# Seven block products in phases of two and five, and one more matrix group of each feed-forward computed that way

## The chip, the cores and the metric

The program runs on one core of a Trainium2 chip. The metric is device time in microseconds of one execution; lower is better. The kernel before takes 2251.7 us (median of three runs, 2251.38 to 2252.15).

## The reference

The reference is one layer of a decoder on 256 rows of 2048 float32 values: a feed-forward block, a token mixer, and a second feed-forward block. The change touches the two feed-forward blocks only. Each computes, with `D_FF` = 5504:

```
def swiglu(x, w_gate, w_up, w_down):
    return (jax.nn.silu(x @ w_gate) * (x @ w_up)) @ w_down
...
    h = swiglu(rms_norm(x, ffn1_pre[l]), ffn1_wg[l], ffn1_wu[l], ffn1_wd[l])
    x = x + 0.5 * rms_norm(h, ffn1_post[l])
```

## The kernel before

All matrix products run on TensorE (PE) in a reduced float32 format. To keep float32 accuracy each operand is split into a high and a low part, and a product is three matmuls: high by high, high by low, low by high. The activations are split once; the weights come from memory as plain float32 (`raw` tiles of 128 x 1024, 512 KB), and for each tile ScalarE (ACT) writes the high part `whi` (L168) and VectorE (DVE) subtracts it to get the low part `wlo` (L169). There are 12 `raw` buffers and 5 pairs of `whi`/`wlo`, so ACT and DVE can be at most five tiles ahead of PE. PSUM has eight banks (`acc`, `tp`), each of 512 columns.

The 43 column tiles of 128 in `D_FF` are worked in five groups of eight (f = 0, 8, 16, 24, 32) and a last group of three. For a group there is a gate product (with `wg`), an up product (with `wu`), the product of both, its transposition (`split_T`, eight transposes on PE a row block, then a split by ACT and DVE into `hh`, `hl`), and a down product (with `wd`) whose partial sums are added in memory (`ysum`, by DMAs of the POOL queue).

A plain product (`linear_steps`) of a group's 1024 columns needs 192 matmuls of 512 columns for the 256 rows. The gate groups f = 8 to 32 use `seven` instead: rows and columns are cut into halves, and the four block products of each quarter are had from seven instead of eight products of sums of blocks, M1 to M7, 168 matmuls. The sums of the activations (`forms`, tiles `sh`, `sl`) are made once. The sums of weight blocks are made per tile: by DVE additions in place (L420, L424), and one by a DMA that adds while it lands (L428, POOL queue). The products run in `phase`s; a phase works on several products side by side, in four steps s = 0 to 3 of two contraction tiles each, and each product holds a PSUM bank until it is done and folded into the results `c0`, `c1`. Before, the phases are M1, M5, M6, M4 and then M3, M2, M7.

`seven` yields after each weight tile (6 matmuls). `weave` takes steps of a main sequence (up and down of group f, 12 matmuls a weight tile) and lets the seven products of the next gate group run in between, in a fixed ratio of matmuls. So the order on each engine is fixed when the program is built; the queues are then worked in order. Loads are issued by the SP queue in that order too. After the woven groups come the up product of f = 32 (plain, two chunks of 512 columns at once) and gate and up of the last three column tiles (one loop with two chunks of 384 columns), both unwoven, and last the down product of the remaining eleven tiles, whose results go through the norm (`closer`).

The functions that are changed, with the line numbers of the profile:

Of the kernel before, what the change touches and what calls it, by code (L numbers as in the profile page):

```python
# [11 lines left out]
F32R = mybir.dt.float32r  # L12
I32 = mybir.dt.int32
AF = mybir.ActivationFunctionType
# [40 lines left out]
def layer(ctx: ExitStack, tc: tile.TileContext, a, out: bass.AP):  # L55
# [17 lines left out]
    def tmp(shape, s="t"):  # L73
        return pool.tile(shape, F32, tag="tmp", bufs=N_TMP, name=nm(s))
# [183 lines left out]
        for _ in linear_steps(*args, **how):  # L258
            pass

    def weave(main, side, ratio):

        credit = 0.0
        for n in main:
            credit += n * ratio
            while side is not None and credit >= 0:
                n = next(side, None)
                if n is None:
                    side = None
                else:  # L270
                    credit -= n
        for n in side or ():
            pass

    def linear_steps(lhs, wts, evac, head=2, tail=4, by_chunk=None, before=None, ahead=None):

        nk, chunks, span, parts = wts.nk, wts.chunks, wts.span, wts.parts
        batches = [min(head, nk)]
        while sum(batches) < nk:
            left = nk - sum(batches)
            batches.append(left if left <= tail else min(2, left - tail))
        ps = [None, None]
        k0 = 0
        for bi, nb in enumerate(batches):
            last = bi == len(batches) - 1
            if before is not None:  # L290
                before(k0)
            wts.need(k0 + nb)
            if last and ahead is not None:
                ahead()
            for t in range(2):
                if bi == 0:
                    while t and pending:
                        pending.pop(0)()
                    ps[t] = [acc(w) for _, _, w in chunks]
                whole = [list(range(len(chunks)))]  # L300
                for cs in ([[c] for c in whole[0]] if last and by_chunk else whole):
# [77 lines left out]
    def seven(forms, W, col, evac):  # L379


        c0, c1 = slot([P, 1024], F32, "sg"), slot([P, 1024], F32, "sg")
        a, b = slice(0, 512), slice(512, 1024)

        def src(i, j, s):
            k = 8 * i + 2 * s
            return W[k * P:(k + 2) * P, col + 512 * j:col + 512 * j + 512].rearrange("(k p) c -> p k c", p=P)

        def load(i, j, s):
            x = raw_tile()  # L390
            nc.sync.dma_start(out=x.rearrange("p (k c) -> p k c", c=512), in_=src(i, j, s))
            return x

        def phase(plan):

            bank = {}
            seen = {p: 0 for p, _, _ in plan}
            for _, p, s, operand in sorted((len(plan) * s + d, p, s, o) for s in range(4) for p, d, o in plan):
                x = operand(s)
                hi, lo = split_tiles()  # L400
                split(hi, lo, x)
                if p not in bank:
                    bank[p] = acc(512)
                ah, al = forms[p]
                for i in range(2):
                    k, ws = 2 * s + i, slice(512 * i, 512 * i + 512)
                    PE.matmul(bank[p], ah[:, k, :], hi[:, ws], start=(seen[p] == 0), stop=False)  # L407
                    PE.matmul(bank[p], ah[:, k, :], lo[:, ws], start=False, stop=False)  # L408
                    PE.matmul(bank[p], al[:, k, :], hi[:, ws], start=False, stop=(seen[p] == 7))  # L409
                    seen[p] += 1  # L410
                yield p if seen[p] == 8 else 0, bank[p]

        xs, es, ys = {}, {}, {}

        def b11(s):
            xs[s], es[s], ys[s] = load(0, 0, s), load(0, 1, s), load(1, 1, s)
            return xs[s]

        def t1(s):
            V.tensor_tensor(xs[s], xs[s], es[s], ALU.add)  # L420
            return xs[s]

        def t2(s):
            V.tensor_tensor(xs[s], xs[s], ys[s], ALU.add)  # L424
            return xs[s]

        def t4(s):
            G.dma_start(out=xs[s].rearrange("p (k c) -> p k c", c=512), in_=src(1, 0, s), accum_op=ALU.add)  # L428
            return xs[s]

        for p, ps in phase([(1, 0, b11), (5, 2.1, t1), (6, 4.2, t2), (4, 8.3, t4)]):
            if p == 1:
                S.activation(c0[:, a], ps, AF.Copy)
            elif p == 5:
                m5 = ps
            elif p == 6:
                q = tmp([P, 512], "q")
                V.tensor_tensor(q, c0[:, a], ps, ALU.subtract)
                V.tensor_tensor(c1[:, b], q, m5, ALU.add)
            elif p == 4:  # L440
                V.tensor_tensor(c1[:, a], q, ps, ALU.add)
            yield 6

        def b22(s):
            xs[s], es[s] = load(1, 1, s), load(0, 1, s)
            return xs[s]

        def b21(s):
            return load(1, 0, s)

        for p, ps in phase([(3, 0, b22), (2, 1, b21), (7, 2.1, t1)]):
            if p == 3:
                V.tensor_tensor(c0[:, b], c1[:, b], ps, ALU.add)
            elif p == 2:
                V.tensor_tensor(c0[:, a], c0[:, a], ps, ALU.add)
            elif p == 7:
                V.tensor_tensor(c1[:, b], c1[:, b], ps, ALU.add)
                V.tensor_tensor(c1[:, a], c1[:, a], ps, ALU.add)
            yield 6
        evac([c0, c1])  # L460
# [107 lines left out]
    def ffn(u, r, first, head, wg, wu, wd, gpost, resid, keep, gname, final, unscale=None):  # L568
# [15 lines left out]
        def chunks(W, f, n):  # L584
            return [(W, c * P, min(512, (f + n - c) * P)) for c in range(f, f + n, 4)]

        def both_later(todo):
            def later():
                for x in todo:
                    x()  # L590

            return later

        def gate_plain(t, ps, f):
            sg[f][t] = slot([P, 1024], F32, "sg")
            for i, p in enumerate(ps):
                S.activation(sg[f][t][:, i * 512:i * 512 + p.shape[-1]], p, AF.Silu, scale=scale(t))
# [21 lines left out]
        def up_steps(f):  # L619
            for i in (0, 4):  # L620
                yield from linear_steps(lu, Weights(KD, [(wu, (f + i) * P, 512)]), lambda t, ps, i=i: up(t, ps[0], f, i, 4))
# [19 lines left out]
        last = n_tile // BLOCK * BLOCK  # L641
        sg = {f: {} for f in range(0, n_tile, BLOCK)}
        forms = {}
        weave(linear_steps(lu, first, lambda t, ps: gate_plain(t, ps, 0), head=head), new_forms(u, forms), 0.5)
        for f in range(0, last, BLOCK):
            if f + BLOCK < last:
                main = itertools.chain(up_steps(f), down_steps(f))
                weave(main, seven(forms, wg, (f + BLOCK) * P, lambda c, f=f + BLOCK: gate_seven(c, f)), 168 / 384)
            else:
                linear(lu, Weights(KD, chunks(wu, f, BLOCK)), lambda t, ps, f=f: both_later([up(t, ps[i], f, 4 * i, 4) for i in range(2)]))  # L650

        def both(t, ps):
            gate_plain(t, ps[:1], last)
            return up(t, ps[1], last, 0, n_tile - last)

        linear(lu, Weights(KD, chunks(wg, last, n_tile - last) + chunks(wu, last, n_tile - last)), both)
        y = [[slot([P, 1024], F32, "y") for _ in range(2)] for _ in range(2)]
        begin, chunk, post, un, rn, sq, _ = closer(y, gpost, 0.5, resid, keep, gname, final, None, unscale)
        f0 = last - BLOCK
        for half in range(2):  # L660
            for t in range(2):
                G.dma_start(out=y[t][half], in_=ysum[t * P:(t + 1) * P, half * 1024:(half + 1) * 1024])
# [504 lines left out]
```

## Time and profile before

| | |
|---|---|
| median of three runs | 2251.7 us |
| the profiled execution | 2252.43 us, span of its instructions 2250.6 us |
| mean granted TensorE clock | 0.993 of full speed |
| busy: PE, weight loads (PEld), DVE, ACT, POOL | 98%, 84%, 67%, 53%, 6% of the span |
| first feed-forward, from its first woven group to its last product | about 85 to 771 us of the span |
| second feed-forward, likewise | about 1564 to 2231 us |

A busy share is the time in which an engine had an instruction running. The durations of single matmuls in the profile are modelled and overlap each other, so the time that one costs is read from the starts of neighbours, not from its own duration.

### The profile page before, as it was taken

What the parts mean: (1) busy time and instruction counts of PE and PEld (TensorE: products, weight loads), DVE (VectorE), ACT (ScalarE), POOL (GpSimd) and SP (SyncE); (2) the same over time, 40 slices, a digit from 0 to 9 for tenths busy, and PEclk for the clock granted to TensorE, in tenths of its full rate; (3) what the DMA queues carried; (4) which work ended last, traced back from release to release, by engine and by line L of the source; (5) the groups of instructions that cost most, each with busy time, mean ns of one, the idle gap of its engine ahead of it and who ended that gap; (6) DMA issues with size and microseconds to landing.
All of it is one profiled execution on the core that took longest, in us unless ns stands there. A gap on an engine that the chain in (4) does not pass through costs nothing.

```text
span 2250.6 us, 28724 instructions
## 1 busy us (share of the span) xinstructions
PE 2211.6 (98%) x10482; PEld 1884.0 (84%) x10482; DVE 1511.4 (67%) x1797; ACT 1203.4 (53%) x1534; POOL 128.7 (6%) x169
## 2 busy tenths in 40 slices
PE   8899999999999999999999999999999999999997
PEld 6788888888889799999888888887888888888896
DVE  5777777767755758676555545558777777776556
ACT  7655556565544654545444444456555565555444
POOL 1000001010000000000000000000000010000100
PEclk9999999999999999999999999999999999999999
DMA  8578889898977464456655566755788898989871
GB/s 301 182 225 271 271 250 280 246 281 257 260 258 260 151 209 128 147 158 179 198 186 189 187 196 204 234 181 172 243 262 277 241 287 246 285 253 273 280 229 54
DMA packets 230016, 505.83 MB, mean 225 GB/s; under 512 B 19129, under 2 KB 52113, under 8 KB 229873
## 3 DMA queue, kind: packets, MB, share of 16 engines
q1 hardware_dynamic: 206400, 448.91, 61.0%
q0 software_dynamic: 23296, 55.00, 11.6%
q8 instruction: 82, 1.34, 0.2%
q14 instruction: 62, 0.50, 0.1%
q10 hardware_dynamic: 176, 0.07, 0.0%
HBM read 480.83 MB, written 23.07 MB: 224 GB/s over the span
## 4 chain that ended last, share of the span: by engine, by line
PE 51%; DVE 1%; ACT 1%; issue 0%; DVEq 0%
PE acc L307 14%; PE acc L308 14%; PE acc L310 14%; PE acc L407 2%; PE acc L409 2%; PE acc L408 2%; PE tp L175 1%; ACT junk L164 0%; ACT uh L186 0%; DVE y L548 0%; DVE raw L352 0%; DVE wlo L169 0%; PE tp L1037 0%; DVE y L526 0%; ACT whi L168 0%
## 5 line engine op out<-in xcount | busy, mean ns | idle before, releaser
L169 DVE TENSOR_TENSOR wlo<-raw,whi 128x1024 fp32r<-128x1024 f32 (+2 forms) x914 | 1068.0, 1180 | 601.5 <-ACT whi L168 576.8
L168 ACT ACTIVATE whi<-raw 128x1024 fp32r<-128x1024 f32 (+2 forms) x914 | 931.1, 1028 | 820.4 <-PE acc L310 675.4
L307 PE MATMUL acc<-whi,uh 128*128 128x512 f32 (+1 forms) x1752 | 657.8, 377 | 11.3 <-ACT whi L168 10.5
L308 PE MATMUL acc<-wlo,uh 128*128 128x512 f32 (+1 forms) x1752 | 652.6, 374 | 2.6 <-DVE wlo L169 2.0
L310 PE MATMUL acc<-whi,ul 128*128 128x512 f32 (+1 forms) x1752 | 555.5, 373 | 0.0
L307 PEld LDWEIGHTS acc<-whi,uh 128*128 128x128 f32 x1752 | 330.0, 189 | 58.8 <-ACT whi L168 12.3
L308 PEld LDWEIGHTS acc<-wlo,uh 128*128 128x128 f32 x1752 | 330.3, 189 | 50.3 <-DVE wlo L169 3.9
L310 PEld LDWEIGHTS acc<-whi,ul 128*128 128x128 f32 x1752 | 326.4, 189 | 46.6
L307 PE MATMUL acc<-whi,hh 128*128 128x512 f32 x688 | 268.9, 391 | 0.0
L308 PE MATMUL acc<-wlo,hh 128*128 128x512 f32 x688 | 267.9, 389 | 0.0
L310 PE MATMUL acc<-whi,hl 128*128 128x512 f32 x688 | 259.4, 389 | 0.0
L310 PEld LDWEIGHTS acc<-whi,hl 128*128 128x128 f32 x688 | 129.2, 188 | 27.0
L308 PEld LDWEIGHTS acc<-wlo,hh 128*128 128x128 f32 x688 | 129.2, 188 | 26.3
L307 PEld LDWEIGHTS acc<-whi,hh 128*128 128x128 f32 x688 | 129.2, 188 | 26.4
L407 PE MATMUL acc<-whi,sh 128*128 128x512 f32 x256 | 101.1, 395 | 0.0
L409 PE MATMUL acc<-whi,sl 128*128 128x512 f32 x256 | 99.8, 390 | 0.0
L408 PE MATMUL acc<-wlo,sh 128*128 128x512 f32 x256 | 99.7, 389 | 0.0
L420 DVE TENSOR_TENSOR raw<-raw,raw 128x1024 f32<-128x1024 f32 x64 | 78.1, 1220 | 0.8
L407 PE MATMUL acc<-whi,uh 128*128 128x512 f32 x192 | 74.9, 390 | 0.0
L409 PE MATMUL acc<-whi,ul 128*128 128x512 f32 x192 | 74.8, 390 | 0.0
L408 PE MATMUL acc<-wlo,uh 128*128 128x512 f32 x192 | 74.7, 389 | 0.0
L428 POOL DMA_DIRECT2D raw<-in_ffn_wg_dram x32 | 38.8, 1213 | 566.6 <-DVE wlo L169 348.8
(321 smaller groups left out, 1862.0 us busy)
## 6 DMA issues: line engine op xcount, KB each, us to landing
raw<-in_ffn_wg_dram SPq DMA_DIRECT2D x224, 512.0 KB, 5.1
raw<-in_ffn_wd_dram SPq DMA_DIRECT2D x172, 512.0 KB, 5.0
raw<-in_ffn_wu_dram SPq DMA_DIRECT2D x160, 512.0 KB, 5.2
raw<-in_w_gate_dram SPq DMA_DIRECT2D x96, 512.0 KB, 4.3
raw<-in_w_in_dram SPq DMA_DIRECT2D x192, 192.0 KB, 3.0
raw<-in_ffn_wg_dram POOLq DMA_DIRECT2D x32, 512.0 KB, 7.5
ysum<-part POOLq DMA_DIRECT2D x64, 256.0 KB, 5.8
raw<-in_w_o_dram SPq DMA_DIRECT2D x32, 512.0 KB, 4.8
```

The costliest lines, as they stand in the source:

```text
L168: S.activation(hi, src, AF.Copy)
L169: V.tensor_tensor(lo, src, f32(hi), ALU.subtract)
L175: PE.transpose(p[:, i, :], src[:, i * P:(i + 1) * P], ident)
L307: PE.matmul(ps[t][c], lh, wh[:, sl], start=(k == 0), stop=False)
L308: PE.matmul(ps[t][c], lh, wl[:, sl], start=False, stop=False)
L310: PE.matmul(ps[t][c], ll, wh[:, span[c]], start=False, stop=(k == nk - 1))
L407: PE.matmul(bank[p], ah[:, k, :], hi[:, ws], start=(seen[p] == 0), stop=False)
L408: PE.matmul(bank[p], ah[:, k, :], lo[:, ws], start=False, stop=False)
L409: PE.matmul(bank[p], al[:, k, :], hi[:, ws], start=False, stop=(seen[p] == 7))
L420: V.tensor_tensor(xs[s], xs[s], es[s], ALU.add)
L428: G.dma_start(out=xs[s].rearrange("p (k c) -> p k c", c=512), in_=src(1, 0, s), accum_op=ALU.add)
```

## The change

In `seven` the phases become (M1, M2) and (M5, M3, M6, M7, M4). Per step the first phase loads two weight tiles, the second three and the accumulating DMA's one; before it was three and one, and then three. The three in-place additions of a step (now all of line 425) stand in the second phase. Five banks are held in the second phase, where it was four and three.

In `ffn` the up product of f = 32 also becomes a `seven` (`up_last`). The plain products that are left (up and down of f = 0 to 24, then gate and up of the last three column tiles, now one after the other with one chunk of 384 columns each) form one main sequence, and all five `seven`s of a feed-forward form one side sequence, woven at half a side matmul for each main matmul: one side tile of 6 matmuls after each main tile of 12. A gate group that is not done when its up product starts is finished first. `run_soon()` is called at the end of the weave.

```diff
-    def weave(main, side, ratio):
+    def weave(main, sides, ratio):
+        sides = list(sides)
         credit = 0.0
+        def one():
+            n = next(sides[0], None)
+            if n is None:
+                sides.pop(0)
+            return n or 0
         for n in main:
+            if not isinstance(n, int):
+                while n in sides:
+                    credit -= one()
+                continue
             credit += n * ratio
...
+            while sides and credit > 0:
+                credit -= one()
+        while sides:
+            one()
...
-        for p, ps in phase([(1, 0, b11), (5, 2.1, t1), (6, 4.2, t2), (4, 8.3, t4)]):
...
-        for p, ps in phase([(3, 0, b22), (2, 1, b21), (7, 2.1, t1)]):
...
+        for p, ps in phase([(1, 0, lambda s: load(0, 0, s)), (2, 1, lambda s: load(1, 0, s))]):
+            if p == 1:
+                S.activation(c1[:, a], ps, AF.Copy)
+            elif p == 2:
+                V.tensor_tensor(c0[:, a], c1[:, a], ps, ALU.add)
+            yield 6
+        def t1(s):
             xs[s], es[s], ys[s] = load(0, 0, s), load(0, 1, s), load(1, 1, s)
+            return add(xs[s], es[s])
         def t4(s):
             G.dma_start(out=xs[s].rearrange("p (k c) -> p k c", c=512), in_=src(1, 0, s), accum_op=ALU.add)
             return xs[s]
+        for p, ps in phase([(5, 0, t1), (3, 1.1, lambda s: ys[s]), (6, 2.2, lambda s: add(xs[s], ys[s])),
+                            (7, 3.3, lambda s: add(ys[s], es[s])), (4, 8.4, t4)]):
+            if p == 5:
                 m5 = ps
+            elif p == 3:
+                m3 = ps
             elif p == 6:
+                V.tensor_tensor(c1[:, a], c1[:, a], ps, ALU.subtract)
+                V.tensor_tensor(c1[:, b], c1[:, a], m5, ALU.add)
+                V.tensor_tensor(c0[:, b], c1[:, b], m3, ALU.add)
             elif p == 7:
                 V.tensor_tensor(c1[:, b], c1[:, b], ps, ALU.add)
+                V.tensor_tensor(c1[:, a], c1[:, a], ps, ALU.add)
+            elif p == 4:
                 V.tensor_tensor(c1[:, a], c1[:, a], ps, ALU.add)
             yield 6
...
-        for f in range(0, last, BLOCK):
-            if f + BLOCK < last:
-                main = itertools.chain(up_steps(f), down_steps(f))
-                weave(main, seven(forms, wg, (f + BLOCK) * P, lambda c, f=f + BLOCK: gate_seven(c, f)), 168 / 384)
-            else:
-                linear(lu, Weights(KD, chunks(wu, f, BLOCK)), lambda t, ps, f=f: both_later([up(t, ps[i], f, 4 * i, 4) for i in range(2)]))
-        def both(t, ps):
-            gate_plain(t, ps[:1], last)
-            return up(t, ps[1], last, 0, n_tile - last)
-        linear(lu, Weights(KD, chunks(wg, last, n_tile - last) + chunks(wu, last, n_tile - last)), both)
+        def up_seven(c, f):
+            for t in range(2):
+                for i in range(2):
+                    g = sg[f][t][:, i * 512:i * 512 + 512]
+                    V.scalar_tensor_tensor(g, c[t][:, i * 512:i * 512 + 512], scale(t, 1 if i == 0 else -1), g, ALU.mult, ALU.mult)
+            def later():
+                for i in (0, 4):
+                    hT[f + i] = (slot([P, 4, 2, P], F32R, "hh"), slot([P, 4, 2, P], F32R, "hl"))
+                    hh, hl = hT[f + i]
+                    for t in range(2):
+                        split_T(hh[:, :, t, :], hl[:, :, t, :], sg[f][t][:, i * P:(i + 4) * P], 4)
+            soon.append(later)
+        m = n_tile - last
+        sides = {f: seven(forms, wg, f * P, lambda c, f=f: gate_seven(c, f)) for f in range(BLOCK, last, BLOCK)}
         f0 = last - BLOCK
+        up_last = seven(forms, wu, f0 * P, lambda c: up_seven(c, f0))
+        def main():
+            for f in range(0, f0, BLOCK):
+                if f:
+                    yield sides[f]
+                yield from up_steps(f)
+                yield from down_steps(f)
+            yield from linear_steps(lu, Weights(KD, chunks(wg, last, m)), lambda t, ps: gate_plain(t, ps, last))
+            yield from linear_steps(lu, Weights(KD, chunks(wu, last, m)), lambda t, ps: up(t, ps[0], last, 0, m))
+        weave(main(), [*sides.values(), up_last], 0.5)
+        run_soon()
```

Three places of the order on the engines. First DVE, at the first `seven` of the first feed-forward, a step with the in-place additions. Before (lines 420 and 424 add, `wlo` are the low parts of tiles):

```order
L420 TENSOR_TENSOR raw_1110<-raw_1110,raw_1112 128x1024
L169 TENSOR_TENSOR wlo_1147<-raw_1110,whi_1146 128x1024
L169 TENSOR_TENSOR wlo_1160<-raw_1157,whi_1159 128x1024
L169 TENSOR_TENSOR wlo_1182<-raw_1175,whi_1181 128x1024
L169 TENSOR_TENSOR wlo_1194<-raw_1191,whi_1193 128x1024
L424 TENSOR_TENSOR raw_1110<-raw_1110,raw_1114 128x1024
L420 TENSOR_TENSOR raw_1175<-raw_1175,raw_1177 128x1024
L169 TENSOR_TENSOR wlo_1211<-raw_1110,whi_1210 128x1024
L169 TENSOR_TENSOR wlo_1224<-raw_1221,whi_1223 128x1024
L169 TENSOR_TENSOR wlo_1241<-raw_1175,whi_1240 128x1024
L424 TENSOR_TENSOR raw_1175<-raw_1175,raw_1179 128x1024
```

In the changed kernel (line 425 adds):

```order
L169 TENSOR_TENSOR wlo_1860<-raw_1852,whi_1859 128x1024
L425 TENSOR_TENSOR raw_1852<-raw_1852,raw_1856 128x1024
L169 TENSOR_TENSOR wlo_1870<-raw_1856,whi_1869 128x1024
L425 TENSOR_TENSOR raw_1856<-raw_1856,raw_1854 128x1024
L169 TENSOR_TENSOR wlo_1882<-raw_1879,whi_1881 128x1024
L169 TENSOR_TENSOR wlo_1901<-raw_1852,whi_1900 128x1024
L169 TENSOR_TENSOR wlo_1916<-raw_1913,whi_1915 128x1024
L169 TENSOR_TENSOR wlo_1933<-raw_1856,whi_1932 128x1024
L169 TENSOR_TENSOR wlo_1947<-raw_1944,whi_1946 128x1024
L169 TENSOR_TENSOR wlo_1953<-raw_1950,whi_1952 128x1024
```

Three additions stand in one step of five side tiles, where it was two in a step of four; the additions of a step and low parts of other tiles alternate.

Second PE, at the end of the first feed-forward's up products: the last matmuls of the up product of three column tiles (`acc_5486`, `acc_5487`; now `acc_5574`), the transposes of its results for the two row blocks (`tp`, from `sg`), and the first down matmuls (operand `hh`). Before, the first and the second group of transposes:

```order
L310 MATMUL acc_5486<-whi_5728,ul_303 128x384
L310 MATMUL acc_5487<-whi_5728,ul_303 128x384
L175 MATMUL tp_5785<-ident,sg_5756 128x128 x3
L307 MATMUL acc_5819<-whi_5809,hh_5438 128x512
L308 MATMUL acc_5819<-wlo_5810,hh_5438 128x512
```

```order
L310 MATMUL acc_5833<-whi_5815,hl_5439 128x512
L310 MATMUL acc_5834<-whi_5815,hl_5439 128x512
L175 MATMUL tp_5847<-ident,sg_5791 128x128 x3
L307 MATMUL acc_5819<-whi_5855,hh_5438 128x512
L308 MATMUL acc_5819<-wlo_5856,hh_5438 128x512
```

In the changed kernel:

```order
L317 MATMUL acc_5574<-wlo_5766,uh_302 128x384
L319 MATMUL acc_5574<-whi_5765,ul_303 128x384
L175 MATMUL tp_5796<-ident,sg_5518 128x128 x3
L175 MATMUL tp_5803<-ident,sg_5532 128x128 x3
L316 MATMUL acc_5834<-whi_5824,hh_5725 128x512
L317 MATMUL acc_5834<-wlo_5825,hh_5725 128x512
L316 MATMUL acc_5835<-whi_5824,hh_5725 128x512
```

The second group of three transposes stood behind 24 matmuls of the down product; now it stands directly behind the first, ahead of the down product.

Third the POOL queue at the first woven gate group (accumulating loads of weights to `raw`, lines 428 and 440; partial sums to `ysum`). Before:

```order
L428 DMA raw_1110<-in_ffn_wg_dram 128x2x512
L428 DMA raw_1175<-in_ffn_wg_dram 128x2x512
L428 DMA raw_1268<-in_ffn_wg_dram 128x2x512
L428 DMA raw_1428<-in_ffn_wg_dram 128x2x512
L635 DMA ysum_756<-part_1685 128x512
L635 DMA ysum_756<-part_1700 128x512
L635 DMA ysum_756<-part_1819 128x512
L635 DMA ysum_756<-part_1834 128x512
```

In the changed kernel:

```order
L440 DMA raw_1374<-in_ffn_wg_dram 128x2x512
L440 DMA raw_1499<-in_ffn_wg_dram 128x2x512
L440 DMA raw_1670<-in_ffn_wg_dram 128x2x512
L627 DMA ysum_756<-part_1711 128x512
L627 DMA ysum_756<-part_1726 128x512
L627 DMA ysum_756<-part_1834 128x512
L627 DMA ysum_756<-part_1849 128x512
L440 DMA raw_1852<-in_ffn_wg_dram 128x2x512
L627 DMA ysum_756<-part_1968 128x512
L627 DMA ysum_756<-part_1983 128x512
```

The fourth accumulating load of a `seven`, before ahead of all partial sums of the group, now stands behind four of them.

## Rows read from the trace of the kernel before

**Rows 1.** The page: busy time of each engine; granted TensorE clock in 40 slices.
```profile
PE 2211.6 (98%) x10482; PEld 1884.0 (84%) x10482; DVE 1511.4 (67%) x1797; ACT 1203.4 (53%) x1534; POOL 128.7 (6%) x169
PEclk9999999999999999999999999999999999999999
```

**Rows 2.** Waits of PE, whole span: waited for; total us, times, longest.
```profile
PE acc L307 <- ACT whi L168: 10.5, 4, 4.0
PE acc L308 <- DVE wlo L169: 2.0, 2, 1.5
```

**Rows 3.** Three stretches: busy us (x count) by engine; last DMA share, GB/s.
```profile
85.00:771.00 686.00, 686.00 (x3117) 573.52 (x3117) 481.78 (x464) 371.73 (x420) 52.14 (x62) 1.00 0.83 254
1564.00:2231.00 667.00, 667.00 (x3029) 558.04 (x3028) 468.82 (x439) 368.24 (x398) 49.91 (x58) 1.00 0.82 249
330.00:455.00 125.00, 125.00 (x561) 103.49 (x560) 93.02 (x87) 70.27 (x76) 10.90 (x11) 1.00 0.90 267
```

**Rows 4.** PE in time, a woven stretch: start us, us, instruction; 512 columns.
```profile
229.66 0.39 PE L310 MATMUL acc<-whi,hl 128*128 128x512 f32 x1
...
234.88 0.39 PE L308 MATMUL acc<-wlo,hh 128*128 128x512 f32 x1
```

**Rows 5.** PE in time, loop of the last column tiles: 384 columns.
```profile
680.60 0.33 PE L307 MATMUL acc<-whi,uh 128*128 128x384 f32 x1
...
687.88 0.33 PE L307 MATMUL acc<-whi,uh 128*128 128x384 f32 x1
```

**Rows 6.** Groups by form: xcount | busy us, mean ns | idle before.
```profile
L169 DVE TENSOR_TENSOR wlo<-raw,whi 128x1024 fp32r<-128x1024 f32 x770 | 931.7, 1223 | 522.7 <-ACT whi L168 500.4 <-DMA raw<-in_ffn_wg_dram 3.7
L168 ACT ACTIVATE whi<-raw 128x1024 fp32r<-128x1024 f32 x770 | 810.3, 1061 | 680.9 <-PE acc L310 552.4 <-issue 46.7 <-PE acc L409 45.7
L169 DVE TENSOR_TENSOR wlo<-raw,whi 128x768 fp32r<-128x768 f32 x128 | 121.4, 955 | 78.4 <-ACT whi L168 76.1
L420 DVE TENSOR_TENSOR raw<-raw,raw 128x1024 f32<-128x1024 f32 x64 | 78.1, 1220 | 0.8
L169 DVE TENSOR_TENSOR hl<-tp,hh 128x512 fp32r<-128x512 f32 x40 | 27.1, 685 | 1.3 <-ACT hh L168 1.3
L609 DVE SCALAR_TENSOR_TENSOR sg<-acc,sg 128x512 f32<-128x512 f32 x20 | 13.6, 687 | 6.4 <-PE acc L310 6.4
```

**Rows 7.** Waits of ACT and DVE, whole span.
```profile
ACT whi L168 <- PE acc L310: 675.4, 475, 6.0
DVE wlo L169 <- ACT whi L168: 576.8, 384, 5.6
```

**Rows 8.** DMA issues (KB each, median us to landing), and the accumulating line L428.
```profile
raw<-in_ffn_wg_dram SPq DMA_DIRECT2D x224, 512.0 KB, 5.1
raw<-in_ffn_wg_dram POOLq DMA_DIRECT2D x32, 512.0 KB, 7.5
...
L428 POOL DMA_DIRECT2D raw<-in_ffn_wg_dram x32: 1194/1213/1263, 132.5 to 2027.5; - x32
DMA to landing us min/median/max: 5.8/7.5/10.3
```

**Rows 9.** In time: PE ends, DVE reacts; eight transposes; the 384-column form.
```profile
148.85 0.39 PE L310 MATMUL acc<-whi,ul 128*128 128x512 f32 x1
...
149.28 0.69 DVE L609 SCALAR_TENSOR_TENSOR sg<-acc,sg 128x512 f32<-128x512 f32 x1 [0.40 <-PE acc L310]
...
673.62 1.03 PE L175 MATMUL tp<-ident,sg 128*128 128x128 f32 x8
674.40 0.42 PE L307 MATMUL acc<-whi,uh 128*128 128x384 f32 x1
...
705.07 0.56 DVE L609 SCALAR_TENSOR_TENSOR sg<-acc,sg 128x384 f32<-128x384 f32 x1 [2.19 <-ACT sg L597]
```

**Rows 10.** The page, costliest groups: matmuls of the products, first and second.
```profile
L407 PE MATMUL acc<-whi,sh 128*128 128x512 f32 x256 | 101.1, 395 | 0.0
L408 PE MATMUL acc<-wlo,sh 128*128 128x512 f32 x256 | 99.7, 389 | 0.0
```

More of the change, by code (lines that the diff above doesn't have):

```diff
@@ L259, in linear @@
             pass
-    def weave(main, side, ratio):
+    def weave(main, sides, ratio):
+        sides = list(sides)
         credit = 0.0
+        def one():
[3 more added lines that the diff above has]
+            return n or 0
         for n in main:
+            if not isinstance(n, int):
+                while n in sides:
+                    credit -= one()
+                continue
             credit += n * ratio
[L266 to L269, printed above, removed]
-                else:
-                    credit -= n
-        for n in side or ():
-            pass
+            while sides and credit > 0:
+                credit -= one()
+        while sides:
+            one()
     def linear_steps(lhs, wts, evac, head=2, tail=4, by_chunk=None, before=None, ahead=None):
@@ L413, in seven, with add @@
         xs, es, ys = {}, {}, {}
-        def b11(s):
-            xs[s], es[s], ys[s] = load(0, 0, s), load(0, 1, s), load(1, 1, s)
[L417 to L425, printed above, removed]
+        def add(x, y):
+            V.tensor_tensor(x, x, y, ALU.add)
+            return x
+        for p, ps in phase([(1, 0, lambda s: load(0, 0, s)), (2, 1, lambda s: load(1, 0, s))]):
[5 more added lines that the diff above has]
+        def t1(s):
+            xs[s], es[s], ys[s] = load(0, 0, s), load(0, 1, s), load(1, 1, s)
+            return add(xs[s], es[s])
         def t4(s):
@@ L429, in t4 @@
             return xs[s]
-        for p, ps in phase([(1, 0, b11), (5, 2.1, t1), (6, 4.2, t2), (4, 8.3, t4)]):
-            if p == 1:
-                S.activation(c0[:, a], ps, AF.Copy)
-            elif p == 5:
+        for p, ps in phase([(5, 0, t1), (3, 1.1, lambda s: ys[s]), (6, 2.2, lambda s: add(xs[s], ys[s])),
+                            (7, 3.3, lambda s: add(ys[s], es[s])), (4, 8.4, t4)]):
+            if p == 5:
                 m5 = ps
+            elif p == 3:
+                m3 = ps
             elif p == 6:
[L437 to L449, printed above, removed]
-        for p, ps in phase([(3, 0, b22), (2, 1, b21), (7, 2.1, t1)]):
[L452 to L455, printed above, removed]
+                V.tensor_tensor(c1[:, a], c1[:, a], ps, ALU.subtract)
+                V.tensor_tensor(c1[:, b], c1[:, a], m5, ALU.add)
+                V.tensor_tensor(c0[:, b], c1[:, b], m3, ALU.add)
             elif p == 7:
                 V.tensor_tensor(c1[:, b], c1[:, b], ps, ALU.add)
+                V.tensor_tensor(c1[:, a], c1[:, a], ps, ALU.add)
+            elif p == 4:
                 V.tensor_tensor(c1[:, a], c1[:, a], ps, ALU.add)
@@ L585, in chunks @@
             return [(W, c * P, min(512, (f + n - c) * P)) for c in range(f, f + n, 4)]
[L587 to L592, printed above, removed]
         def gate_plain(t, ps, f):
@@ L643, in ffn @@
         forms = {}
-        weave(linear_steps(lu, first, lambda t, ps: gate_plain(t, ps, 0), head=head), new_forms(u, forms), 0.5)
-        for f in range(0, last, BLOCK):
-            if f + BLOCK < last:
-                main = itertools.chain(up_steps(f), down_steps(f))
-                weave(main, seven(forms, wg, (f + BLOCK) * P, lambda c, f=f + BLOCK: gate_seven(c, f)), 168 / 384)
-            else:
-                linear(lu, Weights(KD, chunks(wu, f, BLOCK)), lambda t, ps, f=f: both_later([up(t, ps[i], f, 4 * i, 4) for i in range(2)]))
@@ L652, in both @@
-        def both(t, ps):
-            gate_plain(t, ps[:1], last)
-            return up(t, ps[1], last, 0, n_tile - last)
-        linear(lu, Weights(KD, chunks(wg, last, n_tile - last) + chunks(wu, last, n_tile - last)), both)
+        weave(linear_steps(lu, first, lambda t, ps: gate_plain(t, ps, 0), head=head), [new_forms(u, forms)], 0.5)
+        def up_seven(c, f):
[10 more added lines that the diff above has]
+            soon.append(later)
@@ new lines, in ffn @@
+        m = n_tile - last
+        sides = {f: seven(forms, wg, f * P, lambda c, f=f: gate_seven(c, f)) for f in range(BLOCK, last, BLOCK)}
+        f0 = last - BLOCK
+        up_last = seven(forms, wu, f0 * P, lambda c: up_seven(c, f0))
[7 more added lines that the diff above has]
+            yield from linear_steps(lu, Weights(KD, chunks(wu, last, m)), lambda t, ps: up(t, ps[0], last, 0, m))
@@ L657, in ffn @@
+        weave(main(), [*sides.values(), up_last], 0.5)
+        run_soon()
         y = [[slot([P, 1024], F32, "y") for _ in range(2)] for _ in range(2)]
         begin, chunk, post, un, rn, sq, _ = closer(y, gpost, 0.5, resid, keep, gname, final, None, unscale)
-        f0 = last - BLOCK
         for half in range(2):
```

## Prediction

> **What bounds the kernel now.** I read four views, in this order. First the page's busy times and clock [rows 1]: PE is busy 2211.6 us of a span of 2250.6 us, and the granted clock shows a 9 in all 40 slices, so no slice has a clock to win back. A busy share does not prove that PE is the limit, since matmuls overlap in the records, so next come PE's waits [rows 2]: in the whole execution PE waits 10.5 us for high parts, in four places, and 2.0 us for low parts, in two. Third, the windows [rows 3]: in both feed-forwards (85 to 771 and 1564 to 2231 us) PE is busy in all of the time, while DVE is at 70% (481.78 of 686). So the 39 us in which PE is idle lie outside the stretches that are changed. Fourth, the timelines show what PE's time is made of: 23 steps from start to start take 5.22 us [rows 4], 0.227 us for a matmul of 512 columns, and 42 take 7.28 us [rows 5], 0.173 us for one of 384. By the program the first window holds some 2823 matmuls of 512 columns, 192 of 384 and 102 transposes (0.098 us each: eight in 0.78 us [rows 9]). 2823 x 0.227 + 192 x 0.173 + 102 x 0.098 = 684 us, of 686. So PE issues matmuls back to back there, and a matmul less is 0.227 us less. The reverse view agrees: ACT waits 675 us for PE to free a buffer, and DVE 577 us for ACT [rows 7]; both run ahead until the five weight buffers are full.
>
> **The change part by part.**
>
> *Matmuls.* Per feed-forward the up product of f = 32 goes from 192 to 168 matmuls, so 48 go in all: 48 x 0.227 = 10.9 us off PE's back-to-back time. The gate groups have 168 as before. The tiles become smaller in places (six matmuls instead of twelve; one chunk of 384 instead of two), about 56 more in all. The first matmul of a tile takes 395 ns where the next takes 389 [rows 10]: 56 x 6 ns = 0.3 us more.
>
> *The end of each weave.* The two groups of three transposes now stand next to each other, directly behind the last up matmul. The second group needs the product of the last bank. DVE starts on a bank 0.43 us after the start of the last matmul into it, and a 384-column form takes 0.56 us [rows 9]: ready after 0.99 us. Of this PE fills 0.17 with the matmul itself and 0.29 with the first three transposes. Some 0.5 us is left open, twice: 1.0 us more.
>
> *DVE and ACT work.* Two more products as sevens mean 24 additions more (120 instead of 96; 24 x 1.22 = 29 us), 24 splits more (28 tiles instead of 16 a group; 29 us of DVE, 25 us of ACT [rows 6]) and some 14 foldings of banks (0.69 each, 10 us). That is 68 us more for DVE, 1580 of 2241 us, 70%. I cost it at nothing, and the cover has to hold in the densest place, a step of the phase of five. There five side tiles of 6 and five main tiles of 12 matmuls give PE 90 x 0.227 = 20.4 us. DVE has ten low parts (12.2), three additions (3.7) and some 2.5 foldings (1.7): 17.6 us, 86%. ACT has ten high parts, 10.6 us. In the phase of two DVE has no additions and some 14 us of 20.4. The densest of all are the last steps of `up_last`, beside the 384-column main tiles, some five steps in both feed-forwards: PE 30 x 0.227 + 60 x 0.173 = 17.2 us, DVE 5 x 0.955 + 5 x 1.223 + 3 x 1.22 + 1.7 = 16.2 us. The nearest row of before is a stretch with 93.02 us of DVE in 125.00 us (74%) in which PE lost nothing [rows 3]; at 86% and 94% the trace shows nothing. From below: these engines being off PE's path, the cost can't be under 0. From above: if each addition, its high part and its low part ran one behind the other, a step would take DVE and ACT 3 x (1.22 + 1.06 + 1.22) + 2 x 1.22 + 5 x 1.22 + 1.7 = 20.7 us, 0.3 us over PE's 20.4. I take 0, by the nearest row, and because DVE's order puts low parts of other tiles between an addition and the part that waits for its high part.
>
> *Loads.* A step of a seven has six loads (two, then three and the adding one), where it was seven; a plain group has 16. A feed-forward goes from 4 x 28 + 16 = 128 to 5 x 24 = 120: 16 loads of 512 KB less in both, 8.4 MB. The queues move 254 GB/s at a share of 0.83 [rows 3], and a load lands in 5.1 us [rows 8], while with 12 buffers it is asked for some 17 us before its use by the order. PE shows no wait for a load there [rows 2], so nothing is gained: 0. From above, all 16 at 5.1 us would be 82 us, but that needs PE to wait for them now; so I exclude it.
>
> *The accumulating load of M4.* It can be issued once M6's split has read the tile, and it has until M4: two side tiles, some 54 matmuls or 12.2 us of PE. It takes 1.21 us of issue, 7.5 us to land (10.3 at most [rows 8]) and 1.06 us for the high part: 9.8 us, 12.6 at most. In the last step of each `up_last` the cover is 18 x 0.227 + 36 x 0.173 = 10.3 us. On POOL the fourth of these loads now stands behind four stores of partial sums, whose sources are folded long before it. So 0, and from above two tiles at 2.3 us and some of the others at 0.4, about 5 us.
>
> *PSUM.* The phase of five holds five banks, two are left for the main products and one for transposes; a bank is used again 4.5 us or more after its last matmul by the order. DVE frees one in 0.40 + 0.69 us [rows 9]: 0.
>
> *Sum.* The profiled execution took 2252.43 us, its span 2250.6. 2252.43 - 10.9 + 0.3 + 1.0 = 2242.8. The median of the runs is 0.7 us below the profiled one: 2242.1 us.
>
> **The rivals.**
>
> *DVE becomes the bound in the phase of five.* For it: 86% and 94% of DVE's time are taken, an addition must come before a high part that must come before a low part, and DVE works strictly in order, so one late ACT result holds all low parts behind it. It decides from 20.4 us a step on: there are 40 such steps (ten sevens of four), so 0.24 us lost in each eats the 9.6 us of gain. If the chain above also pays DVE's 0.40 us reaction [rows 9] in each of its three links, a step takes 21.9 us, 1.5 us over: 60 us, 2302 us. If one of three additions lies open in every step, 1.22 x 40 = 49 us: 2291 us. Against it: five weight buffers and 12 raw tiles let DVE work ahead over 577 us of waiting [rows 7]. A milder form, 0.1 to 0.2 us a step or 1 us in the five densest, gives 2246 to 2250 us.
>
> *The accumulating load is late.* In the extreme form all 40 of these come 0.24 us late, which needs 13.1 us or more to land against 10.3 at most; the likelier is a few us: 2244 to 2247.
> [...]
>
> *PE's busy time isn't its limit.* If the spacing of 0.227 us came from something else that remains, such as the weight loads or the feeding of tiles, 48 matmuls would go and the time stay at 2251.7 plus the 1.3 us added, 2253 us.
> The page Perfetto Trace Analysis of the Trainium skill, section Identifying the Most-Contended Engine, says that matmul busy time is a bad measure of the room left, and names the busy share of weight loads instead: here 84% [rows 1]. By it there would be a sixth of room in PE, and this rival would stand. What speaks against it is the spacing from start to start, constant over 23 and 42 matmuls and in proportion to the columns (0.227 / 0.173 = 1.31; 512 / 384 = 1.33).
>
> **How the numbers follow.** A run tells 0.2% (4.5 us) from no change. The forecast, PE bound throughout: 0.80, 2239.5 to 2245 us by itself (the sum within a quarter of its terms). Partial loss on DVE: 0.08, 2246 to 2250. Late load: 0.04, 2244 to 2247. PE not the limit: 0.03, 2253. DVE bound: 0.05, 2270 to 2302. Faster by over 4.5 us means under 2247.2: 0.80 + 0.04 + a third of 0.08 gives 0.87. Same: the rest of the partial loss and most of the third rival, 0.08. Slower: 0.05. The range 2239 to 2249 leaves out about 0.1.
>
> **What the profile after would show.** Right: PE busy in all of the woven stretches, spacing 0.227 us, 48 matmuls fewer, 10 us less span; a wait of about 0.5 us of the transposes at the end of each weave; ACT still waiting hundreds of us for PE; DVE at 70%. Wrong: PE waits for the low parts or high parts of line 169 or 168, dozens of times in the phases of five, or for the accumulating load; or a spacing that has grown. A time over 2247 us with PE gapless would say that the terms of the matmuls are mis-sized; one over 2260 that the step in DVE is.

## The result and the profile after

The changed kernel takes 2265.9 us (median of four runs, 2262.8 to 2269.7) against 2251.9 before: a ratio of 1.006, 95% interval 1.0042 to 1.0079. The forecast was 2242.1 us, range 2239 to 2249, and faster. It is slower, by 0.6%.

The profiled execution has a span of 2267.9 us, 17.3 more. First the page's busy line, then both feed-forwards as windows (length, busy us and count of PE, PEld, DVE, ACT, POOL, then clock, DMA share and rate), which answer to [rows 1, 3]:

```profile
PE 2210.5 (97%) x10434; PEld 1876.2 (83%) x10434; DVE 1566.1 (69%) x1859; ACT 1226.4 (54%) x1560; POOL 139.0 (6%) x177
...
85.00:778.00 693.00, 681.83 (x3077) 565.91 (x3075) 508.05 (x496) 383.41 (x435) 57.27 (x66) 1.00 0.80 244
1571.00:2248.00 677.00, 665.93 (x3000) 553.30 (x2999) 495.99 (x469) 378.41 (x411) 55.10 (x62) 1.00 0.79 240
```

The 48 matmuls are gone (x10434, was x10482), but PE is no longer busy all the time in the woven stretches: 11.2 and 11.1 us are idle. What PE waited for (total us, times, longest), against 2.0 us for DVE before [rows 2]:

```profile
PE acc L317 <- DVE wlo L169: 10.3, 11, 2.1
PE acc L417 <- DVE wlo L169: 7.7, 5, 2.3
PE acc L316 <- ACT whi L168: 6.6, 3, 3.7
PE tp L175 <- DVE sg L601: 5.2, 6, 1.2
PE tp L175 <- DVE sg L642: 2.7, 2, 1.5
```

10.3 + 7.7 + 5.2 + 2.7 = 25.9 us for DVE: low parts, and products that are to be transposed. 21.8 us of this lie in the two windows. DVE itself is busy 69%. It too waited, and for something that no row of before shows:

```profile
ACT whi L168 <- PE acc L319: 596.7, 427, 5.7
DVE raw L425 <- DMA raw<-in_ffn_wg_dram: 100.6, 31, 7.7
DVE raw L425 <- DMA raw<-in_ffn_wu_dram: 32.0, 8, 7.3
```

Line 425 holds the additions. 39 of them waited 132.6 us for loads; the 64 additions of line 420 waited 0.8 us before, for all causes [rows 6]. One of these waits in time, on DVE, SP, PE and ACT (start us, us, instruction, idle time and its cause):

```profile
518.76 1.23 DVE L425 TENSOR_TENSOR raw<-raw,raw 128x1024 f32<-128x1024 f32 x1 [7.70 <-DMA raw<-in_ffn_wg_dram]
519.90 1.22 DVE L169 TENSOR_TENSOR wlo<-raw,whi 128x1024 fp32r<-128x1024 f32 x1
521.15 1.23 DVE L425 TENSOR_TENSOR raw<-raw,raw 128x1024 f32<-128x1024 f32 x1
...
507.68 3.77 SPq L400 DMA_DIRECT2D raw<-in_ffn_wg_dram  x3
...
519.09 0.39 PE L416 MATMUL acc<-whi,sh 128*128 128x512 f32 x1
521.18 0.50 PE L417 MATMUL acc<-wlo,sh 128*128 128x512 f32 x1 [1.70 <-DVE wlo L169]
...
534.55 1.06 ACT L168 ACTIVATE whi<-raw 128x1024 fp32r<-128x1024 f32 x1 [1.66 <-PE acc L319]
```

SP issues the three loads of a step from 507.68 on, as buffers come free. DVE reaches the addition of the first two at 511.1 and stands for 7.70 us until the second has landed. Behind it in DVE's order is a low part that is ready (519.90); PE comes to its tile at 519.1, and waits 1.70 us for it. The result of the addition itself is not wanted until 534.6, when ACT splits it. So DVE waits early for a value that is needed late, and the queue behind it pays.

That is a matter of order. In the code an addition stands directly ahead of its split; the scheduler that writes DVE's order put it further ahead, presumably to where it reckons the loads to be there (how it reckons no run shows). Before, the addition into a tile had to stay behind that tile's low part for M1, which held it in place (1 to 10 rows ahead of its own low part). In the changed kernel M1 has a load of its own, so nothing holds the first addition of a step: nearly all of these 40 stand 10 to 17 DVE rows ahead of their low part. For one of them (into `raw_1852`) the fence ahead of the prediction begins with the low part; the first addition stands 12 rows above it, out of sight there.

### The profile page after: what moved, and what is told of

It reads as the page before. It is cut to its first block, busy times and chain, and to the rows that moved or that the text cites. A ratio compares the mean times of both kernels' runs of the same rounds, so it can differ in the third digit from the quotient of the medians.

```text
span 2267.9 us, 28576 instructions
## 1 busy us (share of the span) xinstructions
PE 2210.5 (97%) x10434; PEld 1876.2 (83%) x10434; DVE 1566.1 (69%) x1859; ACT 1226.4 (54%) x1560; POOL 139.0 (6%) x177
## 4 chain that ended last, share of the span: by engine, by line
PE 46%; DVE 3%; DMA 2%; ACT 1%; issue 1%; DVEq 0%; ACTq 0%
PE acc L317 13%; PE acc L319 12%; PE acc L316 12%; PE acc L417 2%; PE acc L418 2%; PE acc L416 2%; DVE wlo L169 2%; DMA raw<-in_ffn_wg_dram 1%; DMA raw<-in_ffn_wu_dram 1%; PE tp L175 1%; ACT junk L164 0%; DMA raw<-in_ffn_wd_dram 0%; ACT uh L186 0%; ACT whi L168 0%; DVE y L547 0%
## 5 line engine op out<-in xcount | busy, mean ns | idle before, releaser
L168 ACT ACTIVATE whi<-raw 128x1024 fp32r<-128x1024 f32 (+2 forms) x938 | 953.7, 1028 | 805.7 <-PE acc L319 596.7
L316 PE MATMUL acc<-whi,uh 128*128 128x512 f32 (+1 forms) x1624 | 607.5, 376 | 7.5 <-ACT whi L168 6.6
L317 PE MATMUL acc<-wlo,uh 128*128 128x512 f32 (+1 forms) x1624 | 604.4, 373 | 9.4 <-DVE wlo L169 8.8
L319 PE MATMUL acc<-whi,ul 128*128 128x512 f32 (+1 forms) x1624 | 527.2, 372 | 0.0
L317 PEld LDWEIGHTS acc<-wlo,uh 128*128 128x128 f32 x1624 | 306.8, 189 | 57.2 <-DVE wlo L169 15.9
L316 PEld LDWEIGHTS acc<-whi,uh 128*128 128x128 f32 x1624 | 306.4, 189 | 51.3 <-ACT whi L168 8.3
L425 DVE TENSOR_TENSOR raw<-raw,raw 128x1024 f32<-128x1024 f32 x120 | 146.8, 1223 | 133.8 <-DMA raw<-in_ffn_wg_dram 100.6
L417 PE MATMUL acc<-wlo,sh 128*128 128x512 f32 x320 | 125.6, 393 | 7.7 <-DVE wlo L169 7.7
L416 PE MATMUL acc<-whi,sh 128*128 128x512 f32 x320 | 126.9, 397 | 0.0
L418 PE MATMUL acc<-whi,sl 128*128 128x512 f32 x320 | 125.5, 392 | 0.0
```

Of the source, the lines that this page charges most:

```text
L168: S.activation(hi, src, AF.Copy)
L425: V.tensor_tensor(x, x, y, ALU.add)
```

## The experiments

Theory PLACE: the first additions stand too early in DVE's queue. Rivals: WORK (DVE has too much to do in the phase of five), LOADS (the loads are late, wherever the addition stands), and later RATIO.

**Additions held back, three tiles.** `los` lists the low parts in the order of the code; `issue_after` says that an instruction is queued behind another one on the same engine; it adds no work:

```diff
-        V.tensor_tensor(lo, src, f32(hi), ALU.subtract)
+        los.append(V.tensor_tensor(lo, src, f32(hi), ALU.subtract).ins)
...
-            return add(xs[s], es[s])
+            with tc.issue_after(los[-3]): return add(xs[s], es[s])
```

> The changed kernel, with one edit: the first addition of each step of the phase of five (x + e, 40 in all) is queued on DVE behind the low part that is written three tiles ahead of its own. Before this edit it stood 10 to 17 rows ahead of its low part, now 1 to 6. PE's order differs in 8 rows of 9807, loads and work are the same. Theory PLACE (the addition stands too early in DVE's in-order queue, waits there for its loads, 133 us in 39 waits, and low parts and free buffers behind it come late): DVE's wait for loads falls from 133 us to under 10, PE's waits for DVE in the two feed-forwards from 26 us to under 3, time 2241 to 2245 us. Rival WORK (DVE has too much to do in the phase of five, 86% of its time): the same work, so PE's waits stay, 2260 to 2268. Rival LOADS (the loads themselves come too late, by ring and DMA queue, wherever the addition stands): the wait moves to ACT or to the new place, 2258 to 2268.

Measured: 2245.2 us, ratio to before 0.9966 (0.9952 to 0.9979), just over the upper end of PLACE; PE still waits 3.6 us for products to be transposed, where under 3 was expected. In the profile no wait of line 425 for a load is left among the waits. WORK falls: the same work, 20.7 us less. LOADS falls too: the same loads, in the same order. In these kernels the split's lines are 167 and 168.

**Eight tiles instead of three.** `los[-8]`. This is the cleanest of them: the orders of PE, ACT, POOL and of the loads are those of the changed kernel row for row; only on DVE do rows stand elsewhere.

> As the kernel whose first additions are queued three tiles ahead of their low part, but eight tiles ahead: they stand 1 to 12 rows ahead, a third of them 7 to 12. PLACE: a time between the two, as the additions stand between: DVE waits for loads some 10 to 60 us, 2246 to 2258 us. If only the very early ones (13 to 17 rows) cost anything: 2245. If it is not the place but something else that the order of three tiles changed: 2262 to 2268.

Measured: 2241.6 us, 0.9949 (0.9936 to 0.9961). The same place in the program and the whole feed-forwards, and all that is left of DVE's waits:

```profile
512.90 1.22 DVE L168 TENSOR_TENSOR wlo<-raw,whi 128x1024 fp32r<-128x1024 f32 x1 [2.85 <-ACT whi L167]
514.15 1.22 DVE L425 TENSOR_TENSOR raw<-raw,raw 128x1024 f32<-128x1024 f32 x1
515.30 3.49 DVE L168 TENSOR_TENSOR wlo<-raw,whi 128x1024 fp32r<-128x1024 f32 x3
...
85.00:764.00 679.00, 677.90 (x3081) 566.35 (x3080) 510.54 (x495) 384.28 (x433) 57.31 (x66) 1.00 0.83 250
1564.00:2219.00 655.00, 653.19 (x2966) 546.23 (x2965) 490.92 (x462) 374.83 (x407) 55.13 (x62) 1.00 0.81 244
...
DVE raw L425 <- DMA raw<-in_ffn_wu_dram: 1.7, 2, 1.0
```

The addition comes without a wait (514.15), PE idles 2.9 us in the windows instead of 22.2, and the time is 24 us less than the changed kernel's, by the places of additions on DVE alone. My expectation of a time in between was wrong: additions up to 12 rows ahead cost nothing here. But rows alone don't draw the line: in the changed kernel the 16 first additions that stand only 10 to 12 rows ahead waited 41.5 us too. What counts is how long DVE has to wait for the loads. Set beside each other by instruction, the first load of a step had landed a median 1.5 us ahead of the start of its addition in the changed kernel (the addition starts as the second one lands), some 5 to 7 us with eight tiles and some 15 us with three.

**One tile.** `los[-1]`.

> As the kernel with the first addition queued three tiles ahead, but directly behind the low part before its own, so that addition, high part and low part follow each other with little between. PLACE: DVE's waits for loads are gone as well; the chain of addition, high part and low part stands open at 2 to 3 us a step, but DVE and ACT are tiles ahead of PE: 2241 to 2248. WORK: a serial chain in a step that is 86% full makes it worse than the unedited kernel: 2268 to 2300. LOADS: 2258 to 2268.

Measured: 2286.7 us, 1.0155 (1.0141 to 1.0168). The number lies where WORK put it, but not for WORK's reason, and PLACE had not foreseen it: `split` also makes the low parts of transposed products, so at the head of a seven the addition was queued behind one of those (line 168 `hl`):

```profile
154.21 0.60 PE L175 MATMUL tp<-ident,sg 128*128 128x128 f32 x4
158.49 0.51 PE L416 MATMUL acc<-whi,sh 128*128 128x512 f32 x1 [3.68 <-ACT whi L167]
...
155.47 0.69 DVE L168 TENSOR_TENSOR hl<-tp,hh 128x512 fp32r<-128x512 f32 x1 [3.03 <-ACT hh L167]
156.08 1.22 DVE L425 TENSOR_TENSOR raw<-raw,raw 128x1024 f32<-128x1024 f32 x1
158.47 2.36 DVE L168 TENSOR_TENSOR wlo<-raw,whi 128x1024 fp32r<-128x1024 f32 x2 [1.17 <-ACT whi L167]
```

PE's next matmul needs the addition, and the addition stands behind work on the transposes that PE makes just before: PE waits 3.68 us, in eight places 22.4 us in all, six of them of 3.68 us. That is half of the 45 us that part this kernel from the one with eight tiles; a good part of the rest is clock (last section). Too late a place costs as much as too early a one, or more.

**The phases alone.** The new `seven` in the kernel before, nothing else.

> The kernel before with the changed function of the seven products alone (phases of two and five), the up product of f = 32 plain as before: 9855 PE rows as before, 32 first additions, 10 to 17 rows ahead of their low parts in half of the cases of both kinds. PLACE: four fifths of the additions, no gain of matmuls: 32/40 of the 26 us that PE lost: 2252 + 21 = 2268 to 2276 us. WORK: four fifths as well where it is the work in the phase, 2268 to 2276. If the woven up product (384-column steps) were the cause: 2252 to 2256.

Measured: 2254.0 us, 1.0007 (0.9998 to 1.0016). Against the expectation of PLACE: the additions are as early, but DVE waits only 24.6 us for loads, and PE not at all for it.

```profile
DVE raw L416 <- DMA raw<-in_ffn_wg_dram: 24.6, 21, 2.4
```

So an early place alone is not enough; the loads must also be late for it. The time is the one that was given for a rival, the woven up product as the cause; the next run, which has no woven up product either, decides on that.

**The phases alone, woven more densely.** There the ratio goes from `168 / 384` to `0.5`.

> The kernel with the new phases alone (gate groups only, 2254 us, DVE waits for loads 24.6 us), with the weave ratio of the changed kernel, 0.5 instead of 0.4375: a step of the phase of five has 90 matmuls of PE beside it instead of 98.6. First additions as early as before, 8 to 17 rows in half of the cases. If the denser weave is what makes the early additions cost time in the changed kernel: DVE's wait for loads rises towards 100 us and the time to 2262 to 2275. If it is the chain of sevens that follow each other without a pause, or the woven up product: 2252 to 2257.

Measured: 2270.2 us, 1.0073 (1.0059 to 1.0086): 16 us more, as expected if the denser weave is what makes early additions cost time. The woven up product is not needed for it. DVE's waits and one place, where line 416 adds and line 599 empties a bank:

```profile
DVE raw L416 <- DMA raw<-in_ffn_wg_dram: 83.5, 30, 6.3
...
PE acc L307 <- DVE sg L599: 13.2, 8, 2.9
...
314.02 0.69 DVE L599 SCALAR_TENSOR_TENSOR sg<-acc,sg 128x512 f32<-128x512 f32 x1 [0.40 <-PE acc L310]
320.26 1.22 DVE L416 TENSOR_TENSOR raw<-raw,raw 128x1024 f32<-128x1024 f32 x1 [5.55 <-DMA raw<-in_ffn_wg_dram]
321.41 1.22 DVE L169 TENSOR_TENSOR wlo<-raw,whi 128x1024 fp32r<-128x1024 f32 x1
322.54 0.68 DVE L599 SCALAR_TENSOR_TENSOR sg<-acc,sg 128x512 f32<-128x512 f32 x1
```

The denser weave turns early places into waits, and a bank is emptied behind one of them: here PE waits for banks, not for low parts. Whose turn it is behind the addition decides which wait one sees.

**Old phases with the woven up product.**

> The changed kernel with the old phases (M1, M5, M6, M4, then M3, M2, M7), five sevens a feed-forward and the new weave: 48 matmuls fewer, first additions 2 to 7 rows ahead of their low parts, because each must follow the low part of the same tile for M1. PLACE: no wait of DVE for loads, the gain of the forecast: 2241 to 2245 us. WORK: a step has two additions or one instead of three, lighter: 2241 to 2248. LOADS: seven loads a step instead of six, so 2245 to 2260. If the weave of the up product with 384-column tiles were the cause: over 2256.

Measured: 2249.3 us, 0.9988 (0.998 to 0.9997). A little faster than before, but 4 us over the upper end of PLACE; the time lies in the range that was given for LOADS. No addition waits here. In six places PE stands at transposes behind an up product. Ahead of one such place ACT stands before the split of M4, whose accumulating load lands late:

```profile
168.72 1.19 POOL L437 DMA_DIRECT2D raw<-in_ffn_wg_dram  x1 [10.26 <-DVE wlo L169]
...
177.49 2.01 ACT L168 ACTIVATE whi<-raw 128x1024 fp32r<-128x1024 f32 x2 [4.88 <-DMA raw<-in_ffn_wg_dram]
```

In the six places PE waits 9.7 us in all for products that DVE finishes late; for the one shown, ACT's wait is what comes ahead of it. It is the same pattern on another engine, and the prediction's second rival, though in the old phases.

**The end of the weave.** With the additions held back three tiles, the ratio 0.52 and no `run_soon()` behind the weave:

```diff
-        weave(main(), [*sides.values(), up_last], 0.5)
-        run_soon()
+        weave(main(), [*sides.values(), up_last], 0.52)
```

> The kernel whose first additions are queued three tiles ahead, and the end of each weave changed too: weave ratio 0.52 instead of 0.5, so that the last seven is done some nine main tiles before the end instead of four, and no call of run_soon() there, so the last group of three transposes stands behind 24 matmuls of the down product again. In the three-tile kernel PE waits 1.6 us for the transposes behind the last seven and 0.5 us for the last three, in each feed-forward. If these waits are the rest of its distance to the forecast: both gone, 4.3 us less, 2240 to 2242 us. Rival: steps shorter by 2.3% (88 matmuls instead of 90) make DVE late somewhere else: 2245 to 2250.

Measured: 2237.3 us, 0.9929 (0.9917 to 0.9942). That is 7.9 us less than with three tiles alone, more than the 4.3 us of the two waits; what gave the rest was not taken apart. No wait of PE for a product to be transposed is left, and PE is busy in 1332.6 of 1334 us:

```profile
85.00:764.00 679.00, 677.55 (x3081) 566.26 (x3079) 514.15 (x502) 386.21 (x439) 57.38 (x66) 1.00 0.83 250
1564.00:2219.00 655.00, 655.00 (x2977) 548.07 (x2976) 493.10 (x466) 376.51 (x410) 55.21 (x62) 1.00 0.81 243
```

> The two edits that helped together: first additions queued eight tiles ahead (2241.6 us alone, PE's waits in the woven stretches gone but for the end of each weave) and the weave ratio 0.52 without the last run_soon() (2237.3 us with additions three tiles ahead). If the waits at the end of the weave are what is left of the eight-tile kernel (3.6 us in both feed-forwards): 2237 to 2239 us. If the denser steps make additions eight tiles ahead wait for loads again, as ratio 0.5 did for the new phases: 2242 to 2255.

Measured with eight tiles: 2237.7 us, 0.9933 (0.9921 to 0.9946), the same.

> The woven up product with the old phases (2249.3 us) and the new end of the weave (ratio 0.52, no last run_soon()). It had four waits of 2.0 to 3.2 us of the transposes behind up products, since ACT waited 4.9 us for the accumulating load of M4, two tiles behind its issue. If this comes from M4's place in the old phase: the waits stay, 2246 to 2249 us. If it comes from the ratio of 0.5, as for the new phases: they go, 2238 to 2242. If the old phases are as good as the new ones when no wait stands open, the time is that of the additions queued early enough, 2237 to 2239.

Measured with the old phases: 2239.2 us, 0.9937 (0.9923 to 0.9951). PE's waits behind the up products are down from 9.7 to 0.2 us; whether by the ratio or by the end, this run can't tell. The intervals of the last three overlap: no gain of the new phases can be told, once no queue stands still.

**The end alone, additions where the scheduler puts them.** This parts PLACE from RATIO.

> The changed kernel with the end of the weave alone changed (ratio 0.52, no last run_soon()); the first additions stand where the scheduler puts them, half of all first additions to a tile 8 to 17 rows ahead. It asks whether the ratio of exactly 0.5 is the cause, since it moved two other kernels by 10 to 16 us. PLACE: DVE still waits for loads, over 60 us, and the time stays at 2252 to 2266 us, 15 us or more over the same kernel with the additions held back (2237.3 and 2237.7). RATIO (the ratio of 0.5 alone makes loads and steps collide): DVE's wait for loads falls under 30 us and the time to 2237 to 2243 us.

Measured: 2289.2 us, 1.0148 (1.0129 to 1.0168). Same source as the 2237.7 us kernel but for the place of the additions, and 51.5 us slower:

```profile
DVE raw L425 <- DMA raw<-in_ffn_wg_dram: 112.2, 29, 9.0
DVE raw L425 <- DMA raw<-in_ffn_wu_dram: 25.5, 7, 8.1
...
PE acc L317 <- DVE wlo L169: 21.8, 10, 5.4
PE tp L175 <- DVE sg L601: 11.7, 4, 5.0
PE acc L417 <- DVE wlo L169: 6.9, 6, 1.9
```

These waits of PE are 40.4 us, where the kernel of 2237.7 us has 4.2; behind the long ones the clock fell too (last section). RATIO falls: 0.5 is nothing special, and the denser 0.52 does not help as long as the additions stand early. PLACE stands, in these dense weaves; at the sparser `168 / 384` the early place cost nothing. It cost even more here than I had expected (2252 to 2266).

## Why the prediction was wrong

- **The step that failed** is that of DVE's and ACT's work: "I take 0, by the nearest row, and because DVE's order puts low parts of other tiles between an addition and the part that waits for its high part". The work did cost nothing: held back eight tiles, it leaves PE idle 2.9 us. What cost 24 us (2265.9 against 2241.6) was the place of 40 additions in an in-order queue, at this density of the weave. I bounded a step by busy time and by a serial chain of its own instructions, and neither bound contains a wait for a load.
- **The step on loads** gave the cover: "asked for some 17 us before its use by the order". I counted to PE's use of the tile. Its first user was the addition on DVE, a whole step ahead of that: asked for at 507.7 to 510.0, wanted at 511.1. With the eyes on the distance between first addition and low part, the order would have shown the danger: 10 to 17 rows, where it was 1 to 10. That it costs time the order alone does not show, since the phases alone have the same distances and lost nothing.
- **The first rival** named the mechanism half ("one late ACT result holds all low parts behind it") with the wrong trigger, a shortage of DVE time. DVE is busy 69%, as forecast, in a kernel that it slows down; and 2265.9 us lies in none of the ranges given for it (2246 to 2250, 2270 to 2302).
- **Matmuls**: right. PE's spacing, 0.227 us, and the count of 48 held; with the waits gone the time is 2237.3 to 2241.6.
- **PE as the bound**: right where the waits are gone, so the third rival falls. The rule from the Trainium skill's page Perfetto Trace Analysis, section Identifying the Most-Contended Engine, that the busy share of weight loads (beside the share of the peak rate reached) shows the room left, was not borne out: at 2237.3 us it is still 84%, with PE back to back.
- **The end of each weave**: a term was missing. Forecast was 0.5 us twice for the last up product (line 601); in the kernel with eight tiles these waits are 0.7 us in both feed-forwards. The transposes of the last seven (line 642), 24 matmuls behind its end, were not among my terms; they wait 2.2 us.
- **A part of the diff that I left out**: `credit >= 0` became `credit > 0`, which delays the first step of the activation sums at the start of the first feed-forward by one. ACT then makes a high part ahead of the sums. From 76 to 88 us, before and after:

```profile
76.00:88.00 12.00, 7.57 (x28) 5.61 (x27) 10.85 (x11) 5.79 (x6) 0.00 (x0) 0.86 0.32 97
```

```profile
76.00:88.00 12.00, 9.88 (x46) 7.82 (x45) 12.00 (x12) 6.87 (x7) 0.00 (x0) 1.00 0.51 158
```

  18 matmuls more in the same time, 18 x 0.227 = 4.1 us, as the wait is shorter and the clock stays up. With this gain, and the 1.0 us at the ends not lost, the forecast of 2242.1 becomes 2237.0; the kernel without standing queues takes 2237.3. This sum was made after the fact, and the gain at the start was not tried alone, but it goes with the new `weave`: from the 193rd to the 251st matmul of the products (first feed-forward) it is 20.9 to 21.6 us in the three kernels with the old one, 17.2 in seven with the new, and 18.8 to 18.9 in the other two, where the clock fell there all the same.
- **The accumulating load**: no cost of its own was seen with the additions held back, as forecast. Two steps to that were wrong. The time to landing [rows 8] counts from the start of the issue, so 1.21 us stand twice in the sum: 8.6 us and 11.4 at most. And two side tiles lie between M6 and M4 only in the last step; in the others, by the order of the products, it is five or six. The "13.1 us or more" of the second rival does not follow from the sum's own terms either: a load late by 0.24 us takes 12.2 + 0.24 - 1.06 = 11.4 us.
- **The time of the loads** itself went up: to landing 8.9 us for the accumulating ones (7.5 before [rows 8]), 5.9 for SP's of `wg` (5.1). DVE's waits don't explain the former: in the kernel of 2237.3 us, where no addition waits, it is still 8.8 us, and 5.3 for SP's. What does was not taken apart. Nor was it shown why the phases alone escape at the sparser weave; a step there has 98.6 matmuls instead of 90, so loads have some 2 us more.

## What to carry to other kernels

An instruction that waits for a load holds up all that stands behind it in its engine's queue, however late its own result is needed. So ask what stands behind it, and where the load's first user stands, not only the user that the product waits for. When a change removes a dependency, ask what that dependency had held in place; the scheduler is free to use it, and here it did. Where a busy share has room but the bound engine waits, one edge of order (no work, no copy) tells place from work in one run.

## What was not expected of the hardware

Behind some stalls PE was slow for a while. In the kernel with additions one tile back, in the 3 us that follow the stall of 3.68 us, against the 4 us ahead of it:

```profile
150.00:154.00 4.00, 4.00 (x20) 3.27 (x19) 0.92 (x2) 1.23 (x2) 0.00 (x0) 1.00 0.00 2
158.70:161.70 3.00, 2.56 (x6) 1.89 (x6) 3.00 (x3) 2.58 (x3) 0.00 (x0) 0.55 0.00 0
```

The granted clock is 0.55, near the lower of the two levels (1.2 of 2.4 GHz), and a matmul costs 0.43 us instead of 0.227. The clock fell so behind all six stalls of 3.68 us of this kernel: 37.6 us at 0.50 in all, in which 73 matmuls start. At 0.2 us more each that is some 15 us (an estimate); with the 22.4 us of waits it makes 37 of the 45 us by which this kernel is slower than the one with eight tiles. In the kernel of 2289.2 us it is 30.7 us and 66 matmuls, some 13 us. In the changed kernel it happens behind the waits of 1.97 us at 666 us and 2.29 us at 2146 us; behind the shorter ones in the two windows the clock stayed up. So a stall can cost more than its length.
